# Layer B of a two-layer encoder: fewer, wider steps for the norms of queries and keys, the key scaling on GpSimd, and another order of the steps

## The chip, the core and the metric

One core of one Trainium2 chip runs the whole program: TensorE (PE in the views, its weight loads PEld), VectorE (DVE), ScalarE (ACT), GpSimd (POOL) and SyncE (SP). The metric is the device time of one launch in microseconds (us).

## The reference, cut to what matters

Two layers over 1024 tokens of width 1024. Layer A is sparse attention with an MLP. Layer B, where the change is, is attention with 16 heads whose keys and values come from a 256-wide latent `c_kv` and whose queries come from a 384-wide one `c_q`. Everything is float32.

```python
kv = (c_kv @ w_ukv).reshape(b, s, 16, 64 + 64)          # keys without position, values
k = rms_norm(concat([kv[..., :64], k_rope_of_all_heads]), k_gain)   # 96 wide, root mean square per head and token
q = rms_norm((c_q @ w_uq).reshape(b, s, 16, 96), q_gain)
k, q = rope_tail(k, cos, sin), rope_tail(q, cos, sin)   # the last 32 of 96 are rotated
p = softmax(where(key_chunk <= query_chunk, q @ k.T * 96 ** -0.5, -1e30))
out = x + (p @ v) @ w_o                                 # then an MLP of width 4096
```

## The kernel before

Tokens go in 8 blocks of 128. All products are made from a high and a low part of each operand (the helper of L86 copies the high part on ACT and subtracts on DVE or GpSimd for the low one), three products for each. A first phase of layer B (1439 to 1519 us) makes `c_kv` and `c_q`. Then its attention runs over 8 pairs of heads, j = 0 to 7, each in four quarters u = 0 to 3: (half 0, head 0), (half 1, head 0), (half 0, head 1), (half 1, head 1), where a half is four blocks of queries. About 52 us go to one pair, until 1962 us. The output projection and the last MLP follow.

**A quarter.** `logits` of a block: products `blps` (L930, in pieces of at most 512 columns, two buffers), a DVE pass that copies them to `bpr` and takes the row extreme into `bsm` (L931), the exponential on ACT (L934), the reciprocal of its sum on DVE (L935), and the scaling of the row by it on GpSimd (L936). In the next quarter `values` transposes these rows (`bpt`, L949), splits them (`bph`, `bpl`, L86), and multiplies by the values (`bpo`, L954); `output` adds the result to `res` (L963, L964). A transpose `bpt` of four blocks needs the fourth block's row last, that of `bpr_…_3`, 1024 wide in half 1.

**Beside it**, steps for later pairs are spread between those of the quarter, in the order of `plan` (`first_plan` for pair 0):

- `kv_a(j, t2)`: keys and values of pair j for two blocks. Products `pukv` (L744), a copy of the keys to `ktok` (L749), then four ACT squares with a running sum, `ksq` (L755, one for each block and head, each followed by a read of the accumulator), into `bkss`; then the inverse root. `rsqrt` (L77 to L82) is on DVE: `ms`, then `y` = `ms` to the power -1/2 on GpSimd (L78), and three small DVE passes over `t` and one over `y` (L79 to L82). Last the keys are multiplied by it on DVE (L759, 256 elements, and L760, the 128 of the rotated part).
- `kv_b`: transposes of `ktok` (`pkt`, L769) and their split to `kth`, `ktl`.
- `q_a(j, t2)`: products `puq` (L788), copy to `qtok` (L792), four squares `bqsq` (L796) with accumulators. `q_b(j, half)`: inverse roots for four blocks (`ms_bq`, `y_bq`, `t_bq`), scaling and rotation (L807 to L813; on GpSimd for j > 0, else on DVE). `queries_t`: transposes `pqt` (L819).

Each engine works off its own queue in the order in which the instructions stand there; the framework that builds the program fixes that order, and an engine whose next instruction waits does nothing else meanwhile.

## Time and profile before

| | |
|---|---|
| three runs, us | 2758.19, 2761.0, 2764.25; median 2761.0 |
| profiled execution, us from its first to its last instruction | 2760.2 |
| layer B: first phase / attention / output projection / MLP, us | 80 / 443 / 90 / 708 |
| PE busy in these, us | 79.8 / 405.4 / 86.6 / 700.2 |

The page gives the profiled execution's span, 2760.2 us, and no time around it; the median of the runs is 0.8 us above it. A stage in which PE is busy nearly all of the time can be shortened by less PE work alone; elsewhere it is the time that PE stands still that could go, and what it stands still for is in the waits.

### The profile page before, as it was taken

What the parts mean: (1) busy time and instruction counts of PE and PEld (TensorE: products, weight loads), DVE (VectorE), ACT (ScalarE), POOL (GpSimd) and SP (SyncE); (2) the same over time, 40 slices, a digit from 0 to 9 for tenths busy, and PEclk for the clock granted to TensorE, in tenths of its full rate; (3) what the DMA queues carried; (4) which work ended last, traced back from release to release, by engine and by line L of the source; (5) the groups of instructions that cost most, each with busy time, mean ns of one, the idle gap of its engine ahead of it and who ended that gap; (6) DMA issues with size and microseconds to landing.
All of it is one profiled execution on the core that took longest, in us unless ns stands there. A gap on an engine that the chain in (4) does not pass through costs nothing.

```text
span 2760.2 us, 37019 instructions
## 1 busy us (share of the span) xinstructions
...
## 2 busy tenths in 40 slices
...
DMA packets 122295, 173.05 MB, mean 63 GB/s; under 512 B 12752, under 2 KB 101104, under 8 KB 122112
## 3 DMA queue, kind: packets, MB, share of 16 engines
...
q14 instruction: 78, 0.64, 0.1%
...
## 4 chain that ended last, share of the span: by engine, by line
PE 52%; DVE 4%; ACT 2%; DMA 1%; issue 1%; POOL 1%; SPq 0%; DVEq 0%; ACTq 0%; POOLq 0%
PE pd L1175 19%; PE pu L1105 19%; PE pwo L1058 2%; PE blps L930 2%; PE bpo L954 2%; PE puq L788 2%; PE bpt L949 1%; PE pukv L744 1%; PE pcq L847 1%; DVE bpr L931 1%; PE pck L847 1%; ACT bpr L934 1%; PE pwob L1058 0%; PE pqt L819 0%; PE pt_m L114 0%
## 5 line engine op out<-in xcount | busy, mean ns | idle before, releaser
L1176 DVE TENSOR_TENSOR res<-res,pd 128x1024 f32<-128x1024 f32 x256 | 310.7, 1218 | 358.7 <-PE pd L1175 358.7
L86 POOL TENSOR_TENSOR dl<-rd,dh 128x1024 fp32r<-128x1024 f32 x96 | 234.5, 2444 | 771.0 <-ACT dh L86 750.2
L1175 PE MATMUL pd<-dh,hh 128*128 128x512 f32 x1024 | 405.4, 396 | 38.1 <-DVE res L1176 25.2
L1105 PE MATMUL pu<-mxh,uh 128*128 128x512 f32 (+1 forms) x1056 | 407.4, 386 | 1.9 <-DVE mxl L86 1.9
L1105 PE MATMUL pu<-mxh,ul 128*128 128x512 f32 (+1 forms) x1056 | 407.0, 385 | 1.6 <-POOL ul L86 1.6
L1105 PE MATMUL pu<-mxl,uh 128*128 128x512 f32 (+1 forms) x1056 | 406.9, 385 | 0.0
L1175 PE MATMUL pd<-dl,hh 128*128 128x512 f32 x1024 | 401.6, 392 | 0.5 <-POOL dl L86 0.5
L1175 PE MATMUL pd<-dh,hl 128*128 128x512 f32 x1024 | 397.1, 392 | 3.3 <-DVE hl L86 3.0
L86 POOL TENSOR_TENSOR ul<-ru,uh 128x1024 fp32r<-128x1024 f32 x96 | 238.6, 2486 | 200.9 <-ACT uh L86 200.8
L86 ACT CAST dh<-rd 128x1024 fp32r<-128x1024 f32 x96 | 100.8, 1054 | 418.8 <-PE pd L1175 344.3
L1175 PEld LDWEIGHTS pd<-dh,hh 128*128 128x128 f32 x1024 | 193.9, 189 | 90.1 <-DVE res L1176 34.0
L1162 ACT ACTIVATE sq<-pu 128x512 f32<-128x512 f32 (+1 forms) x132 | 77.1, 586 | 437.7 <-PE pu L1105 433.7
L86 DVE TENSOR_TENSOR hl<-sq,hh 128x512 fp32r<-128x512 f32 (+1 forms) x132 | 212.0, 1608 | 74.5 <-ACT hh L86 74.5
L1105 PEld LDWEIGHTS pu<-mxh,uh 128*128 128x128 f32 x1056 | 200.8, 190 | 41.6 <-DVE mxl L86 2.4
L1105 PEld LDWEIGHTS pu<-mxh,ul 128*128 128x128 f32 x1056 | 200.8, 190 | 41.3 <-POOL ul L86 2.0
L1105 PEld LDWEIGHTS pu<-mxl,uh 128*128 128x128 f32 x1056 | 200.7, 190 | 39.5
L1175 PEld LDWEIGHTS pd<-dh,hl 128*128 128x128 f32 x1024 | 193.9, 189 | 46.1 <-DVE hl L86 5.4
L1175 PEld LDWEIGHTS pd<-dl,hh 128*128 128x128 f32 x1024 | 194.1, 190 | 40.3 <-POOL dl L86 0.9
L1163 DVE TENSOR_TENSOR sq<-sq 128x512 f32<-128x512 f32 (+1 forms) x132 | 119.8, 909 | 108.5 <-ACT sq L1162 108.2
L442 DVE TENSOR_SCALAR_CACHE_REDUCE both<-score,cand 128x384 f32<-128x384 f32 (+2 forms) x192 | 181.2, 944 | 4.1
L86 ACT CAST hh<-sq 128x512 fp32r<-128x512 f32 (+1 forms) x132 | 80.2, 608 | 186.2 <-DVE sq L1163 185.4
L936 POOL TENSOR_SCALAR bpr<-bpr,bsm 128x640 f32<-128x640 f32 (+7 forms) x128 | 96.9, 763 | 111.5 <-DVE bsm L935 37.7
(384 smaller groups left out, 6104.7 us busy)
## 6 DMA issues: line engine op xcount, KB each, us to landing
...
```

The costliest lines, as they stand in the source:

```text
L86: return self.nc.scalar.copy(h, src), (engine or self.nc.vector).tensor_sub(l, src, h)
L442: nc.vector.tensor_scalar(scratch[0][0][:, :s.shape[-1]], s, cand[:, j:j + 1], None, op0=ALU.is_ge, op1=ALU.add, accum_out=cnt[:, j:j + 1])
L788: nc.tensor.matmul(ps[:, 192 * u:192 * u + 192], a[:, kb, tsl], b[:, kb], start=(kb == 0 and i == 0), stop=(kb == 2 and i == 2))
L847: nc.tensor.matmul(ps, a[:, kb], b[:, kb], start=(kb == 0 and i == 0), stop=(kb == KB - 1 and i == 2))
L930: nc.tensor.matmul(lps, q[0:rows, tsl], k[0:rows, h, c:c + a], start=(m == 0), stop=(m == 2))
L936: nc.gpsimd.tensor_scalar(pr, pr, sm[:, 3:4], 1.0, op0=ALU.mult, op1=ALU.mult)
L954: nc.tensor.matmul(po[:, c], vals[j][:, sb, h], m[:, c], start=(sb == 0 and n == 0), stop=(sb == nb - 1 and n == 1))
L1105: nc.tensor.matmul(pu, a[:, kb], b[:, kb, c0:c1], start=(kb == 0 and i == 0), stop=(kb == KB - 1 and i == 2))
L1162: nc.scalar.activation(sq, pu, AF.Relu)
L1163: nc.vector.tensor_mul(sq, sq, sq)
L1175: nc.tensor.matmul(pd[:, ns], a[:, tsl], b[:, ns], start=(f == 0 and k == 0), stop=(f == NF - 1 and k == 2))
L1176: nc.vector.tensor_add(res[:, tb], res[:, tb], pd)
```

## The change

In layer B alone, and not in its matrix products:

- `kv_a` and `q_a`: one ACT square over all heads of two blocks (256 or 384 elements) into a wider `sq` tile, without an accumulator, and one DVE `tensor_reduce` over it, in place of four squares with accumulators.
- The rest of `kv_a` becomes a step of its own, `kv_n(j, half)`: one inverse root for four blocks (128x8) in place of two (128x4), then the scaling of the keys of those four blocks, on DVE for pair 0 and on GpSimd for all others. `ktok` has four buffers in place of three.
- `plan` and `first_plan` are written anew around it. `kv_a(j+1, 1)` moves from the third quarter to the second, `kv_n(j+1, 0)` stands at the start of the third, `kv_n(j+1, 1)` in the fourth.
- The program is built with `dynamic_dma_scratch_size=1024`. (Comments and docstrings are gone too; line numbers move by up to 7: L930 becomes L937, L931 L938, L936 L943, L949 L956, L759 and L760 become L768 and L769.)

```diff
-                kt = j2.tile([P, 2, 2, 96], F32, name=f"ktok{j}_{t2}", tag="ktok", bufs=3)
-                ss = j2.tile([P, 2, 2], F32, name=f"bkss{j}_{t2}", tag="bkss")
+                kt = j2.tile([P, 2, 2, 96], F32, name=f"ktok{j}_{t2}", tag="ktok", bufs=4)
+                if t2 % 2 == 0:
+                    sums["k", j, t2 // 2] = j2.tile([P, 4, 2], F32, name=f"bkss{j}_{t2}", tag="bkss")
...
-                for u in range(2):
-                    for h in range(2):
-                        junk = j2.tile([P, 96], F32, name=f"ksq{j}_{t2}_{u}_{h}", tag="junk")
-                        nc.scalar.activation(junk[:, 0:64], kt[:, u, h, 0:64], AF.Square, accum_out=ss[:, u, h:h + 1])
-                nc.vector.tensor_add(ss, ss, krs[:, 2 * t2:2 * t2 + 2].unsqueeze(2).to_broadcast([P, 2, 2]))
-                r = self.rsqrt(j2, ss.rearrange("p a b -> p (a b)"), 4, 96, f"bk{j}_{t2}")
-                r4 = r.rearrange("p (a b) -> p a b", a=2).unsqueeze(3)
-                nc.vector.tensor_tensor(kt[:, :, :, 0:64], kt[:, :, :, 0:64], r4.to_broadcast([P, 2, 2, 64]), op=ALU.mult)
-                nc.vector.tensor_tensor(kt[:, :, :, 64:96], krp[:, 2 * t2:2 * t2 + 2].unsqueeze(2).to_broadcast([P, 2, 2, 32]),
-                                        r4.to_broadcast([P, 2, 2, 32]), op=ALU.mult)
+                sq = j2.tile([P, 2, 2, 64], F32, name=f"ksq{j}_{t2}", tag="junk", padded_shape=[P, 2, 2, 96])
+                nc.scalar.activation(sq, kt[:, :, :, 0:64], AF.Square)
+                b = 2 * (t2 % 2)
+                nc.vector.tensor_reduce(sums["k", j, t2 // 2][:, b:b + 2], sq, axis=AX.X, op=ALU.add)
                 keys[j, t2] = kt
+
+            def kv_n(j, half):
+
+                eng = nc.gpsimd if j > 0 else nc.vector
+                ss = sums.pop(("k", j, half))
+                nc.vector.tensor_add(ss, ss, krs[:, 4 * half:4 * half + 4].unsqueeze(2).to_broadcast([P, 4, 2]))
+                r = self.rsqrt(j2, ss.rearrange("p a b -> p (a b)"), 8, 96, f"bk{j}_{half}").rearrange("p (a b) -> p a b", a=4)
+                for t2 in (2 * half, 2 * half + 1):
+                    kt, b = keys[j, t2], 2 * (t2 % 2)
+                    r4 = r[:, b:b + 2].unsqueeze(3)
+                    eng.tensor_tensor(kt[:, :, :, 0:64], kt[:, :, :, 0:64], r4.to_broadcast([P, 2, 2, 64]), op=ALU.mult)
+                    eng.tensor_tensor(kt[:, :, :, 64:96], krp[:, 2 * t2:2 * t2 + 2].unsqueeze(2).to_broadcast([P, 2, 2, 32]),
+                                      r4.to_broadcast([P, 2, 2, 32]), op=ALU.mult)
...
-                for u in range(2):
-                    for h in range(2):
-                        junk = j2.tile([P, 96], F32, name=f"bqsq{j}_{t2}_{u}_{h}", tag="junk")
-                        nc.scalar.activation(junk, q[:, u, h], AF.Square, accum_out=sums[j, half][:, b + u, h:h + 1])
+                sq = j2.tile([P, 2, 2, 96], F32, name=f"bqsq{j}_{t2}", tag="junk")
+                nc.scalar.activation(sq, q, AF.Square)
+                nc.vector.tensor_reduce(sums[j, half][:, b:b + 2], sq, axis=AX.X, op=ALU.add)
...
-                [(kv_a, 1, 0), (queries_t, 1, 0, 0), (q_a, 2, 1)],
-                [(q_w, 3), (kv_a, 1, 1), (kv_b, 1, 0), (q_b, 2, 0), (queries_t, 1, 1, 0), (q_a, 2, 2)],
-                [(kv_a, 1, 2), (kv_b, 1, 1), (queries_t, 1, 0, 1), (kv_a, 1, 3), (q_a, 2, 3)],
+                [(kv_a, 1, 0), (queries_t, 1, 0, 0), (kv_a, 1, 1), (q_a, 2, 1)],
+                [(kv_n, 1, 0), (q_w, 3), (q_b, 2, 0), (kv_b, 1, 0), (queries_t, 1, 1, 0), (q_a, 2, 2)],
+                [(kv_a, 1, 2), (kv_b, 1, 1), (kv_a, 1, 3), (queries_t, 1, 0, 1), (kv_n, 1, 1), (q_a, 2, 3)],
...
-                0: [(q_b, 0, 1), (kv_a, 0, 3), (kv_b, 0, 2), (q_b, 1, 0), (queries_t, 0, 1, 0), (kv_w, 1), (kv_b, 0, 3), (q_w, 2),
-                    (queries_t, 0, 1, 1)],
-                1: [(q_b, 1, 1), (kv_a, 1, 0), (q_a, 2, 0), (queries_t, 1, 0, 0), (q_a, 2, 1)],
+                0: [(q_b, 0, 1), (kv_a, 0, 3), (kv_n, 0, 1), (q_b, 1, 0), (kv_b, 0, 2), (queries_t, 0, 1, 0), (kv_w, 1), (kv_b, 0, 3),
+                    (q_w, 2), (queries_t, 0, 1, 1)],
+                1: [(q_b, 1, 1), (kv_a, 1, 0), (q_a, 2, 0), (kv_a, 1, 1), (queries_t, 1, 0, 0), (q_a, 2, 1)],
```

In the first phase `kv_n(0, 0)` is put behind `kv_a(0, 1)`.

What this does to the queues is shown at two places of pair 3; pairs 2 to 5 have the same order there. A name gives pair, half, head and block, so `bpr3_1_0_3` is the row of the fourth block of half 1, head 0, of pair 3; the number at its end is the buffer's.

**The start of the third quarter.** On GpSimd before, from the second block of the quarter that ends to the first of the one that begins:

```order
L936 TENSOR_SCALAR bpr3_1_0_1_16873<-bpr3_1_0_1_16873,bsm3_1_0_1_16874 128x768
L78 TENSOR_TENSOR y_bk4_0_16916<-ms_bk4_0_16915,mhalf_65 128x4
L936 TENSOR_SCALAR bpr3_1_0_2_16936<-bpr3_1_0_2_16936,bsm3_1_0_2_16937 128x896
L78 TENSOR_TENSOR y_bq5_0_17177<-ms_bq5_0_17176,mhalf_65 128x8
L936 TENSOR_SCALAR bpr3_1_0_3_16967<-bpr3_1_0_3_16967,bsm3_1_0_3_16968 128x1024
L936 TENSOR_SCALAR bpr3_0_1_0_17021<-bpr3_0_1_0_17021,bsm3_0_1_0_17022 128x128
```

and of the change, the same stretch:

```order
L943 TENSOR_SCALAR bpr3_1_0_1_16600<-bpr3_1_0_1_16600,bsm3_1_0_1_16601 128x768
L78 TENSOR_TENSOR y_bk4_0_16780<-ms_bk4_0_16779,mhalf_65 128x8
L943 TENSOR_SCALAR bpr3_1_0_2_16646<-bpr3_1_0_2_16646,bsm3_1_0_2_16647 128x896
L78 TENSOR_TENSOR y_bq5_0_16849<-ms_bq5_0_16848,mhalf_65 128x8
L768 TENSOR_TENSOR ktok4_0_16628<-ktok4_0_16628,y_bk4_0_16780 128x4x64
L769 TENSOR_TENSOR ktok4_0_16628<-krp_12616,y_bk4_0_16780 128x4x32
L768 TENSOR_TENSOR ktok4_1_16705<-ktok4_1_16705,y_bk4_0_16780 128x4x64
L769 TENSOR_TENSOR ktok4_1_16705<-krp_12616,y_bk4_0_16780 128x4x32
L943 TENSOR_SCALAR bpr3_1_0_3_16677<-bpr3_1_0_3_16677,bsm3_1_0_3_16678 128x1024
L943 TENSOR_SCALAR bpr3_0_1_0_16746<-bpr3_0_1_0_16746,bsm3_0_1_0_16747 128x128
```

Both inverse roots (L78) stand ahead of the scaling of `bpr3_1_0_3` in either; of the change the four key scalings stand there as well, behind `y_bq`.

On PE before, from the last product of that block's logits to the first transpose that reads its row (repeated products left out):

```order
L930 MATMUL blps3_1_0_3_512_16974<-kth1_14073,qtl10_14082 128x512
L954 MATMUL bpo3_0_0_16861<-bpl3_0_0_3_16985,bv3_15884 128x128
L744 MATMUL pukv4_1_17088<-ukh4_16712,ckh_12612 128x256
...
L949 MATMUL bpt3_1_0_1_17067<-ident_58,bpr3_1_0_1_16873 128x128
L744 MATMUL pukv4_1_17088<-ukh4_16712,ckl_12613 128x256
L949 MATMUL bpt3_1_0_2_17126<-ident_58,bpr3_1_0_0_16846 128x128
L949 MATMUL bpt3_1_0_2_17126<-ident_58,bpr3_1_0_1_16873 128x128
L930 MATMUL blps3_0_1_0_0_17023<-kth1_14073,qth01_14077 128x128
...
L930 MATMUL blps3_0_1_2_0_17080<-kth1_14073,qtl01_14081 128x384
L769 MATMUL pkt4_0_17147<-ident_58,ktok4_0_16901 96x128 x4
L930 MATMUL blps3_0_1_3_0_17139<-kth1_14073,qth01_14077 128x512
...
L949 MATMUL bpt3_1_0_0_17032<-ident_58,bpr3_1_0_3_16967 128x128
```

and of the change:

```order
L937 MATMUL blps3_1_0_3_512_16684<-kth1_13995,qtl10_14004 128x512
L937 MATMUL blps3_0_1_0_0_16748<-kth1_13995,qth01_13999 128x128
...
L956 MATMUL bpt3_1_0_3_16864<-ident_58,bpr3_1_0_0_16573 128x128
L956 MATMUL bpt3_1_0_3_16864<-ident_58,bpr3_1_0_2_16646 128x128
L937 MATMUL blps3_0_1_1_0_16770<-kth1_13995,qth01_13999 128x256
...
L937 MATMUL blps3_0_1_2_0_16805<-kth1_13995,qth01_13999 128x384
...
L937 MATMUL blps3_0_1_3_0_16840<-kth1_13995,qth01_13999 128x512
...
L937 MATMUL blps3_1_1_0_0_16957<-kth1_13995,qth11_14001 128x320
...
L956 MATMUL bpt3_1_0_0_16757<-ident_58,bpr3_1_0_3_16677 128x128
```

The 12 products `pukv4_1` and the transposes `pkt4_0` no longer stand in between (the former are now ahead of this stretch, the latter behind it); `blps3_1_1_0_0` has come in.

On DVE before, from the last row pass of that block on:

```order
L931 ISA bpr3_1_0_3_16967,bsm3_1_0_3_16968<-blps3_1_0_3_512_16974,zero_14092,bsm3_1_0_3_16968 128x512
L81 TENSOR_SCALAR t_bk4_0_16917<-t_bk4_0_16917 128x4
L77 TENSOR_SCALAR ms_bq5_0_17176<-bqss5_0_16817 128x8
L82 TENSOR_TENSOR y_bk4_0_16916<-y_bk4_0_16916,t_bk4_0_16917 128x4
L964 TENSOR_TENSOR res_69<-bpo3_0_0_16861,btmp3_0_0_16990 64x4x128
L759 TENSOR_TENSOR ktok4_0_16901<-ktok4_0_16901,y_bk4_0_16916 128x4x64
L935 RECIPROCAL bsm3_1_0_3_16968<-bsm3_1_0_3_16968 128x1
L931 ISA bpr3_0_1_0_17021,bsm3_0_1_0_17022<-blps3_0_1_0_0_17023,zero_14092 128x128
```

and of the change:

```order
L938 ISA bpr3_1_0_3_16677,bsm3_1_0_3_16678<-blps3_1_0_3_512_16684,zero_14014,bsm3_1_0_3_16678 128x512
L803 TENSOR_REDUCE bqss5_0_16549<-bqsq5_1_16743 128x4
L938 ISA bpr3_0_1_0_16746,bsm3_0_1_0_16747<-blps3_0_1_0_0_16748,zero_14014 128x128
L81 TENSOR_SCALAR t_bk4_0_16781<-t_bk4_0_16781 128x8
L77 TENSOR_SCALAR ms_bq5_0_16848<-bqss5_0_16549 128x8
L938 ISA bpr3_0_1_1_16768,bsm3_0_1_1_16769<-blps3_0_1_1_0_16770,zero_14014 128x256
L82 TENSOR_TENSOR y_bk4_0_16780<-y_bk4_0_16780,t_bk4_0_16781 128x8
L942 RECIPROCAL bsm3_1_0_3_16678<-bsm3_1_0_3_16678 128x1
```

A reduction, the next block's row pass and a pass of the keys' chain now stand ahead of `ms_bq`, on which `y_bq` on GpSimd waits.

**The start of the next pair's first quarter.** On GpSimd before and of the change:

```order
L78 TENSOR_TENSOR y_bk4_2_17314<-ms_bk4_2_17313,mhalf_65 128x4
L936 TENSOR_SCALAR bpr3_1_1_2_17356<-bpr3_1_1_2_17356,bsm3_1_1_2_17357 128x896
L78 TENSOR_TENSOR y_bk4_3_17438<-ms_bk4_3_17437,mhalf_65 128x4
L936 TENSOR_SCALAR bpr3_1_1_3_17387<-bpr3_1_1_3_17387,bsm3_1_1_3_17388 128x1024
L936 TENSOR_SCALAR bpr4_0_0_0_17479<-bpr4_0_0_0_17479,bsm4_0_0_0_17480 128x128
L936 TENSOR_SCALAR bpr4_0_0_1_17501<-bpr4_0_0_1_17501,bsm4_0_0_1_17502 128x256
```

```order
L78 TENSOR_TENSOR y_bk4_1_17111<-ms_bk4_1_17110,mhalf_65 128x8
L943 TENSOR_SCALAR bpr3_1_1_2_17035<-bpr3_1_1_2_17035,bsm3_1_1_2_17036 128x896
L768 TENSOR_TENSOR ktok4_2_16995<-ktok4_2_16995,y_bk4_1_17111 128x4x64
L769 TENSOR_TENSOR ktok4_2_16995<-krp_12616,y_bk4_1_17111 128x4x32
L768 TENSOR_TENSOR ktok4_3_17063<-ktok4_3_17063,y_bk4_1_17111 128x4x64
L769 TENSOR_TENSOR ktok4_3_17063<-krp_12616,y_bk4_1_17111 128x4x32
L943 TENSOR_SCALAR bpr3_1_1_3_17086<-bpr3_1_1_3_17086,bsm3_1_1_3_17087 128x1024
L943 TENSOR_SCALAR bpr4_0_0_0_17149<-bpr4_0_0_0_17149,bsm4_0_0_0_17150 128x128
```

One inverse root less, and four key scalings more, stand ahead of the scaling of `bpr3_1_1_3`. On PE 17 of the 18 products `puq5_3`, which stood behind the last product of that block's logits, now stand ahead of it.

## Rows read from the trace of the kernel before

**Rows 1.** The page of the profiled execution: its span.

```profile
span 2760.2 us, 37019 instructions
```

**Rows 2.** The view by stretches: from:to in us from the start, length, then busy us (and instructions) of PE, PEld, DVE, ACT and POOL, the granted TensorE clock as a share of full speed, the DMA share and GB/s. The first is the projections of layer B, the next three its attention from the first pair to the eighth (first pair, second, five steady pairs, the last). The last two are short stretches in the first two pairs.

```profile
1439.00:1519.00 80.00, 79.78 (x574) 79.81 (x575) 50.26 (x223) 39.64 (x159) 17.25 (x27) 0.98 0.01 4
1519.00:1562.00 43.00, 30.45 (x204) 27.52 (x204) 34.39 (x102) 25.52 (x106) 23.90 (x24) 0.84 0.06 15
1562.00:1610.00 48.00, 42.06 (x264) 36.35 (x263) 39.07 (x120) 32.30 (x104) 24.49 (x29) 0.89 0.04 12
1610.00:1862.00 252.00, 242.93 (x1654) 212.38 (x1652) 220.35 (x737) 210.10 (x726) 138.22 (x156) 0.99 0.04 10
1862.00:1962.00 100.00, 89.98 (x523) 73.89 (x524) 78.52 (x240) 72.85 (x182) 51.39 (x47) 0.98 0.16 51
...
1536.00:1548.00 12.00, 6.48 (x27) 5.58 (x28) 9.98 (x16) 2.25 (x5) 10.28 (x11) 0.50 0.08 23
1570.70:1573.70 3.00, 2.99 (x11) 2.59 (x11) 1.74 (x4) 1.90 (x4) 1.11 (x2) 0.50 0.00 0
```

**Rows 3.** The view of waits for 1526 to 1962: engine, tile and line that waited, what it waited for, us in total, times, the longest. The last row is the same view for the five steady pairs alone (1610 to 1862).

```profile
PE blps L930 <- DVE bsm L931: 11.9, 24, 2.9
...
PE blps L930 <- DVE bsm L931: 5.9, 17, 0.7
```

**Rows 4.** The view by tile for 1610 to 1862 (five pairs, 20 passes of kv_a), one row for all instructions that write or read a tile; the columns with a number are busy us (and instructions) of the engines named here: ksq on DVE and ACT; bqsq on ACT; bkss on DVE; t_bk on DVE; t_bq on DVE.

```profile
1610.00:1862.00 252.00, 0.00 (x0) 23.42 (x160) 0.99 0.04 10
1610.00:1862.00 252.00, 24.03 (x157) 0.99 0.04 10
1610.00:1862.00 252.00, 10.10 (x40) 0.99 0.04 10
1610.00:1862.00 252.00, 23.49 (x79) 0.99 0.04 10
1610.00:1862.00 252.00, 7.95 (x36) 0.99 0.04 10
```

**Rows 5.** The view by line and shape for 1610 to 1862: line, engine, operation, out<-in, shape, count | busy us, mean ns of one | idle before. Two copies on ACT, then GpSimd, then DVE.

```profile
L749 ACT COPY ktok<-pukv 128x256 f32<-128x256 f32 x20 | 7.3, 367 | 0.6 <-PE pukv L744 0.4
L792 ACT COPY qtok<-puq 128x384 f32<-128x384 f32 x19 | 9.0, 473 | 3.1 <-PE puq L788 2.8
L807 POOL TENSOR_TENSOR qtok<-qtok,y_bq 128x768 f32<-128x768 f32 x9 | 13.2, 1472 | 1.2 <-DVE ms_bk L77 0.7 <-DVE y_bq L82 0.5
L811 POOL TENSOR_TENSOR qtok<-qtok,tn 128x512 f32<-128x512 f32 x9 | 12.1, 1340 | 0.2
L812 POOL TENSOR_TENSOR qtok<-qtok,tq 128x256 f32<-128x256 f32 x9 | 6.6, 733 | 0.9 <-DVE rot L810 0.9
L759 DVE TENSOR_TENSOR ktok<-ktok,y_bk 128x256 f32<-128x256 f32 x19 | 7.9, 417 | 0.2
L760 DVE TENSOR_TENSOR ktok<-krp,y_bk 128x128 f32<-128x128 f32 x19 | 5.4, 282 | 0.0
L931 DVE CUSTOM_DVE_ANT_0 bpr<-blps,zero 128x384 f32<-128x384 f32 x20 | 11.0, 549 | 0.7 <-PE blps L930 0.5
```

**Rows 6.** The timeline of the first pair, PE and DVE: start, us, engine, line, operation, out<-in, shape, and the idle time ahead of it with what ended it.

```profile
1544.01 1.06 PE L769 MATMUL pkt<-ident,ktok 128*96 128x128 f32 x4 [4.52 <-DVE ktok L760]
1537.56 1.43 DVE L79 TENSOR_TENSOR t_bk<-ms_bk,y_bk 128x4 f32<-128x4 f32 x1 [0.78 <-POOL y_bk L78]
...
1567.12 0.66 PE L949 MATMUL bpt<-ident,bpr 128*128 128x128 f32 x4 [1.21 <-POOL bpr L936]
1570.71 0.64 PE L930 MATMUL blps<-kth,qth 104*128 104x320 f32 x1 [2.94 <-DVE bsm L931]
1567.91 1.47 DVE L759 TENSOR_TENSOR ktok<-ktok,y_bk 128x256 f32<-128x256 f32 x1
```

**Rows 7.** The timeline of a steady pair about the start of its third quarter: PE, DVE, POOL.

```profile
1671.22 0.23 PE L954 MATMUL bpo<-bpl,bv 128*128 128x128 f32 x1
1671.28 0.33 PE L744 MATMUL pukv<-ukh,ckh 128*128 128x256 f32 x1
1672.62 0.38 PE L949 MATMUL bpt<-ident,bpr 128*128 128x128 f32 x2
1674.59 0.44 PE L930 MATMUL blps<-kth,qth 104*128 104x384 f32 x1 [0.26 <-DVE bsm L931]
1676.12 0.50 PE L930 MATMUL blps<-kth,qth 104*128 104x512 f32 x1 [0.23 <-DVE bsm L931]
1676.92 0.49 PE L949 MATMUL bpt<-ident,bpr 128*128 128x128 f32 x3
1672.71 0.16 DVE L77 TENSOR_SCALAR ms_bq<-bqss 128x8 f32<-128x8 f32 x1
1672.96 1.64 POOL L78 TENSOR_TENSOR y_bq<-ms_bq,mhalf 128x8 f32<-128x8 f32 x1 [1.11 <-DVE ms_bq L77]
1674.59 1.13 POOL L936 TENSOR_SCALAR bpr<-bpr,bsm 128x1024 f32<-128x1024 f32 x1
```

**Rows 8.** The timeline about the start of the next pair's first quarter: PE, POOL.

```profile
1696.43 0.29 PE L954 MATMUL bpo<-bpl,bv 128*128 128x256 f32 x1
1701.41 0.49 PE L949 MATMUL bpt<-ident,bpr 128*128 128x128 f32 x3
1699.74 1.13 POOL L936 TENSOR_SCALAR bpr<-bpr,bsm 128x1024 f32<-128x1024 f32 x1
```

4 lines of the change are left out of this document (2 added, 2 removed).

## The prediction

> **What bounds the kernel now.** I read the view by stretches first, since a mean over the program says little here. PE is busy for 79.8 of 80 us in layer B's projections, so the part of the change that falls there (a new `kv_n(0, 0)`, fewer squares) lies under PE and gives nothing [rows 2]; with PE's cover gone it would cost its own microsecond or two on ACT and DVE, which stand at 39.6 and 50.3 of 80. All that can move is the 443 us of attention. There PE stands still for 12.6 us in the first pair, 5.9 in the second, 9.1 in the five steady pairs together (1.8 us each) and 10.0 in the last [rows 2]: 37.6 us, which is the most that could be had, apart from what the clock gives. The waits say for what: row passes on DVE that come late (`bsm`), 11.9 us in all, 5.9 in the steady pairs [rows 3]; and in the first pair single long stalls, 4.5 us for `ktok`, then 1.2 and 2.9 us for a scaled row and for a row pass [rows 6]. The clock adds to it: 1536 to 1548 and 1570.7 to 1573.7, right behind these stalls, run at 0.50, the lower of its two levels [rows 2].
>
> **What the change removes and adds, per pair.** ACT: four squares with their accumulator reads take 23.42/20 = 1.17 us a pass for keys and 24.03/19.6 = 1.22 for queries [rows 4]; four passes of each are 9.6 us. The wide squares are not in the trace; the copies of the same 256 and 384 elements take 0.37 and 0.47 [rows 5], so 3.4 us come back: −6.2 us of 42. DVE: the keys' chain takes (10.10 + 23.49)/20 = 1.68 us, four times 6.7 [rows 4]. Two wide ones, at the queries' price of 7.95/9 = 0.88 plus 0.51 for the first two steps, are 2.8. The scaling that leaves is 4 x 0.70 = 2.8 [rows 5]. Eight reductions of 256 or 384 elements come in, which the trace does not have: not under the 0.28 of a 128-element pass, hardly over the 0.42 and 0.55 of passes of their own size [rows 5], so 2.2 to 3.9; I take 3.4, near the passes of the same size. Net −3.3 us (−2.8 to −4.5) of 44. GpSimd: 128 elements of scaling are not in the trace. A line through `qtok` with 512 and 256 elements (1.34, 0.73) gives 0.73 + 0.43 for a pass of keys; the slope of the 768-element one, whose second operand is repeated in the same way, gives 0.58 + 0.35 [rows 5]. Four instructions are thus 1.85 to 2.33 us; I take 2.1, the middle, as both shapes occur. PE's products stay the same.
>
> The Trainium skill, "GPSIMD Engine Reference", section "Elementwise — side-by-side cycle accounting", has GpSimd 1.96 times as slow as DVE in a two-input pass; by that the four would take 2 x 1.96 x 0.70 = 2.7 us, and the forecast below would be some 4 us longer. The trace's own pairs of sizes say less.
>
> So DVE and ACT, which are late now, get lighter, and GpSimd, busy for 27.6 of 50 us in a steady pair, gets heavier. That would be a plain gain if nothing waited for GpSimd. The order says that something does.
>
> **Third quarter, pairs 2 to 5.** Count from E, when the last product of the fourth block's logits has gone out (1671.22 in the pair shown [rows 7]). Before, `ms_bq` runs at E+1.5, `y_bq` from E+1.74 to E+3.4, the row `bpr_1_0_3` until E+4.5; PE gets to the transposes that need it only at E+5.7, with 0.49 us of idle on the way. The change puts a reduction (about 0.45), a 128-wide pass (about 0.3) and a 0.16 step ahead of `ms_bq`, but no longer a held `t_bk`: `y_bq` starts at E+2.0 to E+2.65, I take E+2.2. Then 1.64 for it, 2.1 for the four key scalings, which now stand ahead of the row, 1.13 for the row: E+7.1. On PE the twelve `pukv` (1.4 us by [rows 7]) and four `pkt` (about 0.4) that filled this time are gone, and about 0.4 of logits came in: it arrives at 5.7 − 1.4 − 0.4 + 0.4 = E+4.3, or E+3.8 if the idle 0.49 goes. It then stands still for about 3.3 us. Less the 0.49 of before: +2.9 us, four times **+11.6**. Bounds: 2.0 with cheap scalings and late PE, 3.9 with dear ones.
>
> **First quarter of the next pair, three times.** The keys' scaling waits for the last step of its chain, which DVE now reaches behind the last pass of the old row, two passes of the new quarter and the `res` sum (estimates by 0.55 for 384 columns [rows 5]: 0.7, 0.3, 0.4 and 0.7, with 0.9 for a chain of four steps and 0.5 of waiting for products in between): about E'+3.5; plus 2.1 and 1.13 is E'+6.7, where the row was done at E'+4.4 before and PE came at E'+5.0 [rows 8]. PE has lost 17 `puq` of cover (1.9 us), but its logits wait for the same row passes. Between 0 (these hold PE as long) and 3.7 I take 1.4, nearer the former: **+4.2**.
>
> **First pair.** `pkt` stood still for 4.5 us because the chain from 1537.56 on was stretched: its first step took 1.43 us, and a scaling at 1567.91 took 1.47, against means of 0.30 and 0.42 [rows 4 to 6]. The new order ends this chain for four blocks at once, ahead of the queries' GpSimd work that lay beside it: −2.5 (−1 to −4). The 1.2 and 2.9 us before 1570.71 came from a chain and two scalings ahead of a row pass; those scalings leave DVE: −3 (0 to −4.1). The lower clock behind it goes with it: 3 us at 0.50 are 1.5 us lost, −1.5. The 3.99 us ahead of it stay, since the queries of pair 0 are not touched. Together **−7**.
>
> **Other waits.** Of 9.1 us in the steady pairs I let the lighter DVE take 3.5, of 10.0 at the end 2.5: **−6** (0 to −14).
>
> **Clock.** Stalls of 2.9 us and more were followed by the lower level [rows 2, 6]. If each second of the four new ones is, at 1.5 us: **+3** (0 to +12).
>
> Sum: 11.6 + 4.2 − 7 − 6 + 3 = +5.8 on the span of 2760.2 [rows 1], so 2766.0; the median of the runs stood 0.8 above the span: **2767 us**. 0.2%, 5.5 us, is about what a measurement of this kernel can tell from no change.
>
> **The rivals.**
> (a) GpSimd holds PE, as above: 2767, its own range 2761 to 2776. Chance 0.38.
> (b) The relief carries, faster: GpSimd gets its scalings done before PE asks, since 1.1 us of idle stood ahead of `y_bq` [rows 7]. It decides at bpr done by E+4.3, which needs the scalings behind the row or `y_bq` 2.8 us earlier; or the first pair gives back far more. Then −7 − 6 and up to −9 more of the idle: 2740 to 2755, about 2748. For it speaks that DVE is what PE waits for now [rows 3]; against it that the order on GpSimd is fixed. Chance 0.34.
> (c) Both cancel: 2756 to 2766. Chance 0.18.
> (d) The clock falls behind every new stall, seven of them at up to 3 us: 2776 to 2790. For it the two stretches at 0.50. Chance 0.10.
> A rule that speaks for (a) or (d): the Trainium skill, "SBUF — State Buffer", section "Who interferes with whom", says that a DVE pass with two SBUF inputs and a GpSimd instruction that reads SBUF block each other, the later one until the first is done. The stretched `t_bk` of 1.43 us agrees [rows 6]. By that rule the queries' chain would run into the four scalings on GpSimd at each head and DVE would give back about 1.2 us each time, two thirds of its relief; the time would be near 2771.
>
> Within 0.2% (2755.5 to 2766.5) are (c) and a quarter of (a): 0.27. Faster: (b) and a little of (c), 0.36. Slower: the rest of (a) and (d), 0.37. The range of 2746 to 2782 leaves out the lower third of (b) and the upper half of (d).
>
> **What the next profile would show.** Right: PE waits for `bpr` on GpSimd at the transposes grow from 1.2 us to 10 or more, in single stalls of about 3 us at the third quarters of pairs 2 to 5; DVE in 1610 to 1862 falls from 44 to about 41 a pair, ACT from 42 to 36, GpSimd rises to about 31; `pkt` no longer waits 4.5 us in the first pair. Wrong: no such stalls, `y_bq` early or the key scalings far under 1.85 us for four, PE idle in the steady pairs under 1.8 us each.

## The result, and the profile after

The changed kernel takes **2788.9 us** (median of 4 runs, 2783.1 to 2790.1) against 2761.7 of the kernel before (4 runs, 2758.2 to 2764.3) beside it: 1.0100 times as long, 95% interval 1.0087 to 1.0112. The forecast was 2767 within 2746 to 2782. The sign of its likeliest case was right, with 0.37 given to slower and 0.36 to faster; the time lies above the range.

The page of the profiled run gives its span, which answers to [rows 1]: 27.8 us more.

```profile
span 2788.0 us, 36514 instructions
```

The view by stretches (from:to, length, busy us and instructions of PE, PEld, DVE, ACT and POOL, granted clock, DMA share, GB/s), first of after: from the first logits of pair 2 to the first of pair 6, and the whole attention. Then of before: the whole attention and pairs 2 to 5, cut at the same instructions.

```profile
1649.00:1876.00 227.00, 205.50 (x1341) 178.57 (x1340) 184.95 (x555) 149.69 (x361) 125.24 (x153) 0.95 0.04 10
1533.00:1993.00 460.00, 409.50 (x2587) 353.95 (x2586) 365.57 (x1095) 302.06 (x715) 256.09 (x295) 0.94 0.07 20
```

```profile
1529.00:1963.00 434.00, 399.36 (x2589) 344.66 (x2588) 365.27 (x1179) 334.57 (x1086) 236.00 (x253) 0.96 0.07 20
1646.00:1852.00 206.00, 198.24 (x1342) 172.57 (x1341) 180.54 (x597) 169.69 (x576) 114.92 (x128) 0.99 0.04 11
```

The attention is 26 us longer. PE does the same products (2587 records, 2589 before), so its 10.1 us of extra busy time are slower products (granted clock 0.94 for 0.96), and the other 15.9 us are idle time (50.5 for 34.6, each the length less PE's busy time). In pairs 2 to 5 the split is 7.3 and 13.7 of 21 us. ACT has become lighter by 32.5 us in the attention; DVE's busy time has not moved in all (365.6 for 365.3); in pairs 2 to 5, which take 21 us more, it rose by 4.4 us (185.0 for 180.5).

The waits of PE in 1526 to 2000, and the first row of the same view for pairs 2 to 5 (1649 to 1876). Before, `bpt` waited for `bpr` once, for 1.2 us [rows 6], and the longest sum was the 11.9 us for `bsm` [rows 3].

```profile
PE bpt L956 <- POOL bpr L943: 17.7, 13, 2.9
PE blps L937 <- DVE bsm L938: 8.5, 17, 1.5
...
PE pkt L777 <- DVE ktok L769: 5.8, 1, 5.8
...
PE bpt L956 <- POOL bpr L943: 14.5, 8, 2.9
```

One of these stalls, at the start of the third quarter of pair 3 (the place of [rows 7], one pair on): PE, then DVE, then POOL.

```profile
1735.21 0.23 PE L937 MATMUL blps<-kth,qth 104*128 104x128 f32 x1
...
1739.21 0.31 PE L937 MATMUL blps<-kth,qtl 96*128 96x320 f32 x1
1742.10 0.86 PE L956 MATMUL bpt<-ident,bpr 128*128 128x128 f32 x4 [2.58 <-POOL bpr L943]
1743.80 0.63 PE L961 MATMUL bpo<-bph,bv 128*128 128x512 f32 x1
1744.22 0.63 PE L961 MATMUL bpo<-bpl,bv 128*128 128x512 f32 x1
...
1737.89 0.16 DVE L942 RECIPROCAL bsm<-bsm 128x1 f32<-128x1 f32 x1
...
1737.43 1.65 POOL L78 TENSOR_TENSOR y_bq<-ms_bq,mhalf 128x8 f32<-128x8 f32 x1 [2.02 <-DVE ms_bq L77]
1739.05 0.61 POOL L768 TENSOR_TENSOR ktok<-ktok,y_bk 128x256 f32<-128x256 f32 x1
1739.62 0.40 POOL L769 TENSOR_TENSOR ktok<-krp,y_bk 128x128 f32<-128x128 f32 x1
1739.97 0.61 POOL L768 TENSOR_TENSOR ktok<-ktok,y_bk 128x256 f32<-128x256 f32 x1
1740.54 0.40 POOL L769 TENSOR_TENSOR ktok<-krp,y_bk 128x128 f32<-128x128 f32 x1
```

The reciprocal of the row's sum is there at 1738.05, but GpSimd has `y_bq` and four scalings ahead of it and takes it at 1740.92; PE stands from 1739.52 to 1742.10. Behind the stall the products of 512 columns come 0.42 us apart, and the granted clock is near 0.50, the lower level (1.2 of 2.4 GHz). It is so behind all four stalls of 2.57 to 2.87 us at the third quarters of pairs 2 to 5 (PE, then the stretches behind them):

```profile
1684.45 1.11 PE L956 MATMUL bpt<-ident,bpr 128*128 128x128 f32 x4 [2.87 <-POOL bpr L943]
1799.92 0.67 PE L956 MATMUL bpt<-ident,bpr 128*128 128x128 f32 x4 [2.58 <-POOL bpr L943]
1856.93 0.66 PE L956 MATMUL bpt<-ident,bpr 128*128 128x128 f32 x4 [2.57 <-POOL bpr L943]
...
1684.50:1687.90 3.40, 3.40 (x13) 2.98 (x14) 2.66 (x6) 2.59 (x6) 3.40 (x6) 0.52 0.00 0
1742.50:1745.90 3.40, 3.40 (x14) 2.73 (x12) 2.67 (x7) 2.92 (x6) 3.40 (x5) 0.51 0.02 5
1800.50:1803.90 3.40, 3.33 (x12) 2.85 (x12) 2.46 (x7) 2.74 (x6) 3.40 (x5) 0.51 0.01 2
1858.50:1861.90 3.40, 3.37 (x13) 2.70 (x12) 2.97 (x6) 2.22 (x5) 3.17 (x4) 0.50 0.02 5
1687.90:1742.50 54.60, 48.98 (x336) 42.55 (x335) 44.64 (x136) 35.62 (x89) 29.11 (x36) 1.00 0.04 11
```

The last row is the time between two of them: with no wait over 1.00 us in it, the clock stays full.

Per shape, in pairs 2 to 5, the new operations cost (DVE, ACT, ACT, DVE, then the two scalings on GpSimd; to be read against [rows 5]; the second figure behind the bar is the mean in ns):

```profile
L803 DVE TENSOR_REDUCE bqss<-bqsq 128x4 f32<-128x384 f32 x16 | 8.7, 547 | 0.2 <-ACT bqsq L802 0.2
L802 ACT ACTIVATE bqsq<-qtok 128x384 f32<-128x384 f32 x15 | 7.9, 524 | 0.3
L754 ACT ACTIVATE ksq<-ktok 128x256 f32<-128x256 f32 x15 | 6.5, 436 | 0.0
L756 DVE TENSOR_REDUCE bkss<-ksq 128x4 f32<-128x256 f32 x15 | 6.1, 408 | 0.0
...
L768 POOL TENSOR_TENSOR ktok<-ktok,y_bk 128x256 f32<-128x256 f32 x16 | 9.8, 612 | 5.9 <-DVE y_bk L82 5.9
L769 POOL TENSOR_TENSOR ktok<-krp,y_bk 128x128 f32<-128x128 f32 x16 | 6.4, 398 | 0.0
```

So the stalls that the prediction's first rival described are there. The question for the experiments was whether they are the 27 us.

### The profile page after: what moved, and what is told of

Its sections match the earlier page's. It is cut to its first block, busy times and chain, and to the rows that moved or that the text cites. A ratio compares the mean times of both kernels' runs of the same rounds, so it can differ in the third digit from the quotient of the medians.

```text
span 2788.0 us, 36514 instructions
## 1 busy us (share of the span) xinstructions
PE 2576.8 (92%) x13354; PEld 2173.9 (78%) x13354; DVE 1874.9 (67%) x3996; ACT 1132.4 (41%) x2409; POOL 1045.6 (38%) x796
## 3 DMA queue, kind: packets, MB, share of 16 engines
q8 instruction: 105, 1.72, 0.3%
## 4 chain that ended last, share of the span: by engine, by line
PE 52%; DVE 4%; POOL 2%; issue 1%; DMA 1%; ACT 1%; SPq 0%; DVEq 0%; ACTq 0%; POOLq 0%
PE pd L1182 18%; PE pu L1112 18%; PE pwo L1065 3%; PE blps L937 2%; PE bpo L961 2%; PE puq L796 2%; PE pukv L744 1%; PE bpt L956 1%; PE pcq L854 1%; PE pck L854 1%; DVE bpr L938 1%; POOL bpr L943 1%; DMA ukr<-in_w_ukv_dram 1%; PE pqt L826 0%; PE pkt L777 0%
## 5 line engine op out<-in xcount | busy, mean ns | idle before, releaser
L1182 PEld LDWEIGHTS pd<-dh,hh 128*128 128x128 f32 x1024 | 194.9, 190 | 90.8 <-DVE res L1183 34.6
L943 POOL TENSOR_SCALAR bpr<-bpr,bsm 128x640 f32<-128x640 f32 (+7 forms) x128 | 94.6, 747 | 102.7 <-DVE bsm L942 59.4
```

What stands on the lines that cost most here:

```text
L943: nc.gpsimd.tensor_scalar(pr, pr, sm[:, 3:4], 1.0, op0=ALU.mult, op1=ALU.mult)
L1182: nc.tensor.matmul(pd[:, ns], a[:, tsl], b[:, ns], start=(f == 0 and k == 0), stop=(f == NF - 1 and k == 2))
```

## The experiments

Ratios are to the kernel before, run beside each, with 95% intervals. Line numbers of a kernel's rows are its own.

**Undo one part of the change at a time.** The first four runs leave out or keep one part each: the scaling on GpSimd, the new order of steps, or all but one.

e1, against the changed kernel:

```diff
-                eng = nc.gpsimd if j > 0 else nc.vector
+                eng = nc.vector
```

> The changed kernel with one word changed: the keys are scaled on DVE for every pair, not on GpSimd for all but the first. Its order on PE about the third quarter's start is that of the changed kernel (no pukv and no pkt between the last logits of the fourth block and the transposes that need its row); on GpSimd only the two inverse roots stand ahead of that row. Theory A (the four scalings on GpSimd ahead of the row hold PE): the row is done 2.0 us earlier at some ten heads, PE's waits for bpr on GpSimd fall from 17.7 us to under 6, the lower clock behind them goes for the most part, and the time is 2764 to 2772. Theory B (the steps' new order took the products away that covered this time, whichever engine scales): 2779 to 2788, since the lost cover stays lost and DVE gets 2.8 us a pair back.

2784.1 us, 1.0087 (1.0071 to 1.0104). With the keys scaled on DVE again PE's waits for GpSimd's rows fall from 17.7 us to 4.4, none over 0.8, but other waits take their place (PE's longest sums in 1526 to 2000; the changed kernel has 8.5 for `bsm`):

```profile
PE blps L937 <- DVE bsm L938: 17.4, 32, 1.5
PE bpt L956 <- DVE ktl L86: 7.0, 6, 1.4
```

By this run the scaling on GpSimd is worth 4 or 5 of the 27 us.

e2, against the changed kernel: the plan of before, with `kv_n` behind each second `kv_a`.

```diff
-                [(kv_a, 1, 0), (queries_t, 1, 0, 0), (kv_a, 1, 1), (q_a, 2, 1)],
-                [(kv_n, 1, 0), (q_w, 3), (q_b, 2, 0), (kv_b, 1, 0), (queries_t, 1, 1, 0), (q_a, 2, 2)],
+                [(kv_a, 1, 0), (queries_t, 1, 0, 0), (q_a, 2, 1)],
+                [(q_w, 3), (kv_a, 1, 1), (kv_n, 1, 0), (kv_b, 1, 0), (q_b, 2, 0), (queries_t, 1, 1, 0), (q_a, 2, 2)],
...
```

> The changed kernel with the plan of before (kv_a in its old places, each kv_n right behind its second kv_a); the scaling stays on GpSimd. Now the scalings stand behind the long rows of both heads on GpSimd, and the twelve pukv cover the third quarter's start again. Theory A and theory B both expect the heads' stalls to be gone: 2752 to 2765. Theory C (GpSimd as such is too full, or its key scalings slow DVE through the memory they share, wherever they stand): 2775 to 2788, with DVE passes of two inputs stretched as much as in the changed kernel.

2790.6 us, 1.0116 (1.0095 to 1.0137): the old plan brings nothing back. Under it the keys come late (PE waits 13.0 us in 9 stalls for `ktok` on GpSimd).

e3, against the kernel before; the keys' squares likewise.

```diff
-                for u in range(2):
-                    for h in range(2):
...
-                        nc.scalar.activation(junk, q[:, u, h], AF.Square, accum_out=sums[j, half][:, b + u, h:h + 1])
+                sq = j2.tile([P, 2, 2, 96], F32, name=f"bqsq{j}_{t2}", tag="junk")
+                nc.scalar.activation(sq, q, AF.Square)
+                nc.vector.tensor_reduce(sums[j, half][:, b:b + 2], sq, axis=AX.X, op=ALU.add)
```

> The kernel before with one part of the change: wide squares on ACT and reductions on DVE, the inverse roots for two blocks, scaling on DVE and plan as before. If the relief of ACT (6.2 us a pair) and the small extra of DVE (3.4 us a pair) are what the first step of the prediction said, it is within 2752 to 2764. If the reductions on DVE delay the row passes, over 2766.

2775.8 us, 1.0059 (1.0041 to 1.0076). The wide squares with their reductions, which I had netted inside DVE's sum, cost 15 us alone.

e4, against the kernel before; the scaling of the other 128 elements likewise.

```diff
-                nc.vector.tensor_tensor(kt[:, :, :, 0:64], kt[:, :, :, 0:64], r4.to_broadcast([P, 2, 2, 64]), op=ALU.mult)
+                eng = nc.gpsimd if j > 0 else nc.vector
+                eng.tensor_tensor(kt[:, :, :, 0:64], kt[:, :, :, 0:64], r4.to_broadcast([P, 2, 2, 64]), op=ALU.mult)
```

> The kernel before with one part of the change: the keys are scaled on GpSimd for all but the first pair, two blocks at a time, plan and squares as before. About the third quarter's start two scalings (1.0 us) stand ahead of the long row on GpSimd, and the twelve pukv still cover it. Theory A: PE reaches the row about when it is done, 2758 to 2768. Theory C: over 2770.

2760.3 us, 1.0000 (0.9991 to 1.0009). Moving 2.8 us a pair from DVE to GpSimd neither costs nor gives anything under the plan of before.

**Squares or reductions, and is a lighter engine worth anything?**

x1, against the kernel before; x4 has the first two lines alone.

```diff
+                red = j2.tile([P, 2, 2], F32, name=f"kred{j}_{t2}", tag="kred")
+                nc.vector.tensor_reduce(red, kt[:, :, :, 0:64], axis=AX.X, op=ALU.add)
...
+                red = j2.tile([P, 2, 2], F32, name=f"qred{j}_{t2}", tag="kred")
+                nc.vector.tensor_reduce(red, q, axis=AX.X, op=ALU.add)
```

> The kernel before with eight more DVE reductions a pair (0.41 and 0.55 us each, 3.8 us a pair), whose results nothing reads; the squares on ACT, the order of the products and all else as before. Theory D (DVE is the engine that PE waits for, and each reduction that stands in its queue ahead of row passes and splits is paid for): 2770 to 2780, as the kernel with squares and reductions (2775.8). Theory O (not DVE's load costs, but the new order of PE's products that the framework makes when ACT's squares get short): 2760 to 2765.

2776.3 us, 1.0062 (1.0046 to 1.0079), as e3: eight reductions a pair that nobody reads cost 17 us, with ACT's squares as they were. What PE waits for (1526 to 2000) is passes on DVE, of which `bpl` has grown (the third row is of before):

```profile
PE bpo L958 <- DVE bpl L86: 10.8, 19, 1.6
PE blps L934 <- DVE bsm L935: 10.7, 17, 2.9
...
PE bpo L954 <- DVE bpl L86: 3.6, 11, 0.7
```

> The kernel before with four more DVE reductions a pair in place of eight, those over the keys (0.41 us each, 1.6 us a pair), results unused. In proportion to eight (3.8 us a pair, 15 us): 2766. If there is slack that the first ones use up: 2760 to 2763.

2770.1 us, 1.0033 (1.0023 to 1.0044): about 10 us for the four of the keys, whose work is 1.6 us a pair by the row of the 256-element reduction above, 13 in all; x1 pays 17 for some 30.

x2 and x3, against the kernel before. x2 has one wide square with one accumulator for all heads of a pass and no reduction; x3 leaves out the 256-element scaling of the keys for all pairs but the first.

```diff
+                s1 = j2.tile([P, 1], F32, name=f"bks1{j}_{t2}", tag="bks1")
+                nc.scalar.activation(sq, kt[:, :, :, 0:64], AF.Square, accum_out=s1)
...
+                if j == 0:
+                    nc.vector.tensor_tensor(kt[:, :, :, 0:64], kt[:, :, :, 0:64], r4.to_broadcast([P, 2, 2, 64]), op=ALU.mult)
```

> The kernel before with one wide square in place of four in each pass and no reductions: the accumulator of the one square stands for all four sums (so the norms of keys and queries in layer B are other numbers than the reference's). DVE's work is that of before, ACT loses about 4.5 us a pair; the twelve pukv still stand behind the fourth block's last logits. Theory D: 2750 to 2760, what the relief of ACT is worth by itself. Theory O: over 2765.

2757.2 us, 0.9995 (0.9984 to 1.0005). In 1610 to 1862 ACT is busy for 185.3 us instead of the 210.1 of [rows 2], and nothing is gained.

> The kernel before without the wider of the two passes that scale the keys (0.42 us, four a pair) for all pairs but the first, so that these keys are not normalised in 64 of 96 columns; nothing takes its place, the order on PE is that of before. If each microsecond of DVE counts alike, up and down: 1.7 us a pair less give 6 to 7 us, 2752 to 2755. If DVE only bounds once more work is put on it: 2757 to 2761.

2763.8 us, 1.0011 (1.0001 to 1.0020). DVE 1.7 us a pair lighter, and no gain. So e4, x2 and x3 give no sign of the "relief" of my sum. They don't show that it is worth nothing: none of them keeps the order of before. Against the trace of before, at least 217, 356 and 170 of PE's 13354 instructions stand in another place, so that a worse order may have eaten a gain.

**The order of single steps.**

e5, against the changed kernel:

```diff
-                [(kv_n, 1, 0), (q_w, 3), (q_b, 2, 0), (kv_b, 1, 0), (queries_t, 1, 1, 0), (q_a, 2, 2)],
+                [(q_w, 3), (q_b, 2, 0), (kv_n, 1, 0), (kv_b, 1, 0), (queries_t, 1, 1, 0), (q_a, 2, 2)],
```

> The changed kernel with one step moved: kv_n of the third quarter stands behind q_b, by which its scalings stand behind the long row on GpSimd there (in the first quarter they still stand ahead). Theory A (the scalings ahead of the row are what costs): the stalls of 2.6 us at the third quarters and the lower clock behind them go, 2770 to 2776. If DVE's reductions and the lost cover cost instead, as the kernel with all keys on DVE says: 2780 to 2790.

2796.8 us, 1.0134 (1.0119 to 1.0149): slower still, and PE's waits for `bpr` on GpSimd stay (18.8 us in 11, for 17.7 in 13).

e7 is e2 with the scaling on DVE; y1 is the kernel before with the keys' roots for four blocks at once and nothing else (accumulators on ACT, scaling on DVE, old plan).

> The changed kernel with the plan of before and all keys scaled on DVE: of the change only squares, reductions and the inverse roots for four blocks are left. Against the kernel with squares and reductions alone (2775.8) it shows what the inverse roots for four blocks cost, against the changed kernel with keys on DVE (2784.1) what the plan costs. If the plan costs: 2772 to 2778. If keys that wait for four blocks cost: 2782 to 2788, with PE waiting for pkt's keys.

2788.0 us, 1.0101 (1.0085 to 1.0116), with 13.4 us of waits for `ktok`, 5.8 of them in one stall that the changed kernel has as well.

> The kernel before with the inverse roots for four blocks alone: squares with accumulators on ACT, no reductions, keys scaled on DVE, plan of before with each kv_n behind its second kv_a. DVE loses about 3.9 us a pair (two chains of 1.4 in place of four of 1.7). If DVE's load is all that counts (15 us for 3.8 us a pair more): about 2745. Theory W (keys that wait for the second two blocks come late for their transposes, and the chain, the scalings and the queries' chain fall together): 2766 to 2775, with PE waiting for keys at pkt.

2770.4 us, 1.0038 (1.0028 to 1.0049), with 15.7 us in 12 waits of `pkt` for `ktok` (6.1 in 2 before): under the old plan, keys that wait for four blocks come late. The new plan is there to mend that.

y2, against the changed kernel; the queries' squares likewise.

```diff
-                sq = j2.tile([P, 2, 2, 64], F32, name=f"ksq{j}_{t2}", tag="junk", padded_shape=[P, 2, 2, 96])
-                nc.scalar.activation(sq, kt[:, :, :, 0:64], AF.Square)
...
-                nc.vector.tensor_reduce(sums["k", j, t2 // 2][:, b:b + 2], sq, axis=AX.X, op=ALU.add)
+                for u in range(2):
+                    for h in range(2):
...
+                        nc.scalar.activation(junk[:, 0:64], kt[:, u, h, 0:64], AF.Square, accum_out=sums["k", j, t2 // 2][:, b + u, h:h + 1])
```

> The whole change but for one part: the four squares with accumulators stay on ACT, so that there are no reductions on DVE. If the reductions' 15 us add to the rest: 2770 to 2776. If the rest alone is as slow (the scalings on GpSimd ahead of the long rows, the new plan): over 2780. If the change is good but for the reductions: under 2757.

2763.9 us, 1.0017 (1.0008 to 1.0027). Everything else in the change costs 4 or 5 us; with the wide squares and their reductions it costs 27. The build option `dynamic_dma_scratch_size` is in y2 and in x2 as well, so it is not the loss. At the place of the stall shown above, GpSimd now takes the row first (POOL, DVE, PE of y2):

```profile
1726.38 1.13 POOL L945 TENSOR_SCALAR bpr<-bpr,bsm 128x1024 f32<-128x1024 f32 x1 [1.07 <-DVE bsm L944]
1727.61 0.61 POOL L769 TENSOR_TENSOR ktok<-ktok,y_bk 128x256 f32<-128x256 f32 x1
...
1729.82 1.65 POOL L78 TENSOR_TENSOR y_bq<-ms_bq,mhalf 128x8 f32<-128x8 f32 x1
...
1729.19 0.34 DVE L77 TENSOR_SCALAR ms_bq<-bqss 128x8 f32<-128x8 f32 x1
...
1727.57 0.66 PE L958 MATMUL bpt<-ident,bpr 128*128 128x128 f32 x4
```

But the source of y2 does not say so: its steps stand in the same plan. The framework that records the kernel orders the instructions of each engine itself, and with eight instructions a pair more on DVE and fewer on ACT it had made another order on every engine: in the traces of y2 and of the change at least 376 of PE's 13354 instructions and 66 of GpSimd's 796 stand in different places. So the runs up to here mix two causes, DVE's work and the order.

**Work and order apart.** At the end of the recording each instruction gets an edge to the one that is to stand ahead of it on its engine (order only, no wait), from a table of another kernel's order; the reductions alone are free. In this way f1 has x1's reductions in the order of before, g1 the order of x1 and no reduction, f2 the changed kernel in y2's order, and g2 y2 in the changed kernel's order. In the traces each of the four has on PE, DVE, ACT and GpSimd the sequence that it was to have, instruction by instruction, reductions and squares apart.

```diff
+        order = ORDER[e]
+        row = [i for u in order for i in us[u]]
+        for a, b in zip(row, row[1:]):
+            tc.add_manual_dep(b, a.name, no_sync, reason="impose")
```

> The kernel before with eight unused reductions a pair on DVE, as in x1 (2776.3 us), but with the instructions of PE, DVE, ACT and GpSimd held in exactly the order that they have in the kernel before; only the reductions are new among them. Load theory (the 3.8 us of reductions a pair on DVE make the row passes late): about 2776 us, ratio 1.006, and PE waits for bpl and bsm on DVE as in x1 (10.8 and 10.7 us). Order theory (the framework puts the products of layer B in a worse order once the reductions are there): 2760 us, ratio 1.000.

2765.1 us, 1.0021 (1.0011 to 1.0031). PE's waits for `bpl` are near those of before: 4.3 us in 12, for 3.6 in 11.

> The other half of the same test: the kernel before without any reduction, its instructions on the four engines held in the order that they have in x1. Load theory: about 2760 us, ratio 1.000. Order theory: about 2776 us, ratio 1.006. If both halves lie between, each cause has the share that its half shows.

2769.3 us, 1.0035 (1.0022 to 1.0049). Of x1's 17 us about 6 are work on DVE and about 10 the order. The waits for `bpl` that x1 seemed to owe to its reductions are here without one:

```profile
PE bpo L954 <- DVE bpl L86: 10.1, 17, 1.6
```

No run holds a kernel in its own order alone, so what the edges themselves cost is not measured; f1's 6 and g1's 10 us together don't exceed x1's 17, which leaves them little.

> The changed kernel with its reductions and wide squares, its instructions held in the order that they have in y2_change_without_reductions (2763.9 us), so that on GpSimd the scalings of the keys stand behind the row bpr at the third quarter. Load theory: near the changed kernel's 2788 us, ratio 1.010. Order theory: near 2764 us, ratio 1.002.

2771.7 us, 1.0041 (1.0026 to 1.0056): with the reductions, in y2's order, 7 us over y2 and 17 under the changed kernel.

> y2 (accumulators on ACT, no reduction on DVE) with its instructions held in the order of the changed kernel, so that the scalings of the keys stand ahead of the row bpr at the third quarter. Load theory: near 2764 us, ratio 1.002. Order theory: near 2788 us, ratio 1.010, with stalls of some 2.6 us for bpr on GpSimd at the heads of the third quarter.

2789.7 us, 1.0107 (1.0092 to 1.0122): the changed kernel's order costs the whole 27 us without a single reduction, 25 us more than y2. Its longest sum of waits in 1526 to 2000 is that of the changed kernel (17.7 us in 13):

```profile
PE bpt L958 <- POOL bpr L945: 17.9, 14, 2.9
PE blps L939 <- DVE bsm L940: 11.8, 20, 1.5
```

**Is it the four stalls at GpSimd's row?** The last two runs keep the changed kernel's own order and move four instructions of GpSimd, the rows `bpr2_1_0_3` to `bpr5_1_0_3`: in h3 ahead of `y_bq` and the scalings, in h4 between them.

In GpSimd's order, h3 for pair 3:

```diff
 L943 TENSOR_SCALAR bpr3_1_0_2<-bpr3_1_0_2,bsm3_1_0_2 128x896
+L943 TENSOR_SCALAR bpr3_1_0_3<-bpr3_1_0_3,bsm3_1_0_3 128x1024
 L78 TENSOR_TENSOR y_bq5_0<-ms_bq5_0,mhalf 128x8
 L768 TENSOR_TENSOR ktok4_0<-ktok4_0,y_bk4_0 128x4x64
...
-L943 TENSOR_SCALAR bpr3_1_0_3<-bpr3_1_0_3,bsm3_1_0_3 128x1024
```

> The changed kernel (2788 us) held in its own order, with one thing moved: at the third quarters of pairs 2 to 5, GpSimd's row bpr_1_0_3 stands ahead of y_bq and the four scalings instead of behind them, four instructions moved in all. Nothing moves on PE, DVE or ACT. Theory that GpSimd's order at these four places is the loss: the row starts at about 1738.05 instead of 1740.92 in the pair whose stall ends at 1742.10, the four stalls of up to 2.6 us and the lower clock behind them go, so 2770 to 2776 us, ratio 1.004 to 1.006. Theory that the order of the products on PE is the loss: 2784 to 2788 us, ratio 1.009 to 1.010.

2789.1 us, 1.0115 (1.0098 to 1.0132): nothing comes back. GpSimd's row is in time now, and PE stands still longer one step on, behind the four transposes (PE, DVE, POOL of h3 at the same place):

```profile
1733.99 0.64 PE L937 MATMUL blps<-kth,qth 104*128 104x320 f32 x1 [3.45 <-DVE bsm L938]
...
1731.47 0.57 DVE L79 TENSOR_TENSOR t_bq<-ms_bq,y_bq 128x8 f32<-128x8 f32 x1 [1.98 <-POOL y_bq L78]
1732.43 0.54 DVE L81 TENSOR_SCALAR t_bq<-t_bq 128x8 f32<-128x8 f32 x1
1733.25 0.68 DVE L938 CUSTOM_DVE_ANT_0 bpr<-blps,zero 128x512 f32<-128x512 f32 x1
...
1728.71 1.12 POOL L943 TENSOR_SCALAR bpr<-bpr,bsm 128x1024 f32<-128x1024 f32 x1 [2.73 <-DVE bsm L942]
1729.80 1.65 POOL L78 TENSOR_TENSOR y_bq<-ms_bq,mhalf 128x8 f32<-128x8 f32 x1
```

The row pass on DVE that frees the bank for the next logits stands behind the queries' chain (`t_bq`, three more steps), and its first step waits for `y_bq`, now the later one on GpSimd: 1.98 us of idle DVE and 1.8 of chain, ahead of a pass that PE waits for. The stall is the queries' inverse root on two in-order queues; which of the two ends it depends on what stands first on GpSimd.

> As h3, but the row stands behind y_bq and ahead of the four scalings alone, so that only what the change put there (2.02 us of scalings) is moved, and y_bq (1.65 us) stays ahead as in the kernel before. Theory that the scalings ahead of the row are the loss: the four stalls shrink from about 2.6 to 0.6 us, 8 us of idle and some of the lower clock come back, 2774 to 2780 us, ratio 1.005 to 1.007. Theory of the products on PE: 2784 to 2788 us.

2789.6 us, 1.0115 (1.0099 to 1.0130). The stall for `bpr` falls to 0.72 us; one of 0.91 for the row pass and one of 3.03 for `bpl` on DVE come in behind it, the last of these:

```profile
1743.43 0.50 PE L961 MATMUL bpo<-bpl,bv 128*128 128x512 f32 x1 [3.03 <-DVE bpl L86]
```

**What stays open.** Most of the loss is the order of the instructions, as g2 and f2 show, and moving four places on GpSimd alone gives none of it back, as h3 and h4 show. Which places make it is open: whether the place of the chain on DVE would give it back, or that of the products on PE, which no longer cover it, was not tried. Why the framework's order comes out so once reductions are there is not in the trace.

## Why the prediction was right or wrong

Two steps of the prediction failed. It counted a lighter DVE ("Net −3.3 us") as time that PE gets back, and outside the two places that it read it took the order of the instructions to stay as it was (pair 1 at nothing, the last pairs at −2.5). The runs show that the new order costs 25 us without a reduction (g2 against y2), and that DVE did not get lighter.

The forecast's sum against the trace, by the time of the first logits of a pair (1529.13 and 1532.86 for pair 0, before and after; 1592.55 and 1590.17 for pair 1; 1646.39 and 1648.66 for pair 2; 1851.94 and 1876.21 for pair 6; last value product 1963.15 and 1993.11). The stretches of [rows 2] are not cut there: 1562 to 1610, called the second pair, is the end of pair 0 and the start of pair 1, and 1610 to 1862 goes from pair 1 into pair 6.

| stretch | forecast, us | measured, us |
| --- | --- | --- |
| up to pair 0 | 0 | +3.7, of which 2.4 ahead of layer B's projections |
| pair 0 | −7 | −6.1 |
| pair 1 | 0 | +4.7 |
| pairs 2 to 5 | +11.6 +4.2 −3.5 +3 = +15.3 | +22.0 |
| pairs 6 and 7 | −2.5 | +5.7 |
| behind the attention | 0 | −2.1 |
| sum | +5.8 | +27.9 |

Of the first row, what lies ahead of the projections is no work of the change: up to there both programs run the same products in the same order. Single executions differ so; in h3 and h4, which share that part, pair 0 begins at 1523.9 and 1527.2.

- **Third and first quarters, +11.6 and +4.2: right in place, releaser and size.** PE waits for `bpr` on GpSimd 14.5 us in pairs 2 to 5, against 15.8. They are four stalls of 2.6 to 2.9 us at the third quarters (2.9 was forecast, four scalings of 2.02 for 2.1) and four of 1.0 at the first quarters (three of 1.4). With the slower products, 7.3 us, they make up nearly all that these pairs lost. The forecast has a slip here: 3.3 less 0.49 is 2.8, so its term should be 11.2. In the stall shown, with E at 1735.21, `y_bq` starts at E+2.2 (the value taken), PE comes at E+4.3 (the same) and the row is done at E+6.8 (7.1). It does not follow that the scalings are the cause of the loss: with them on DVE (e1, in another order again) the time falls by 5 us, with them behind the row (h3, h4) not at all. Rival (b) put the point from which the relief would carry at a row done by E+4.3; in h3 it is done 4.1 us after E, and nothing carries.
- **"Net −3.3 us" of DVE a pair: the first step that failed.** The prices of the new operations were right (reductions 3.8 a pair, forecast 3.4 with 3.9 as the bound; squares 0.52 and 0.44 for 0.47 and 0.37), but DVE did not get lighter. In pairs 2 to 5 it is busy for 46.2 us a pair, 45.1 before. Its passes for the queries, which run beside GpSimd's (last section), became dearer: the four steps of their chain take 1.48 us for 0.86 and the two passes of the rotation 1.72 for 0.98, 2.7 us a pair more in all. The second pass of the rotation after, and before:

```profile
L817 DVE TENSOR_TENSOR rot<-qtok,sgq 128x128 f32<-128x128 f32 x8 | 8.8, 1095 | 0.0
L810 DVE TENSOR_TENSOR rot<-qtok,sgq 128x128 f32<-128x128 f32 x8 | 3.3, 418 | 0.0
```

  Nor can work in a queue taken in order be netted; it counts by its place. The reductions cost 6 us in the order of before (f1), 7 in x1's (x1 against g1) and 7 in y2's (f2 against y2), and nothing in the change's own (the change against g2); in the last two cases ACT's lighter squares came with them.
- **"Other waits, −6": wrong in sign, the second step that failed.** Pair 1 and pairs 6 and 7, which I priced at 0 and −2.5, lost 4.7 and 5.7. The sum took the order of the rows it quoted at two places and let the rest of the program stand as it was. The change had moved instructions on every engine, and this order costs 25 us without the reductions (g2 against y2) and 17 with them (the change against f2). In y2's order the work on DVE is about 7 us (f2 against y2). The two don't add up; that the stalls of the order hide the work is likely, but not shown.
- **Clock, +3: mis-sized.** Slower products cost 10.1 us in the attention, 7.3 of them in pairs 2 to 5. The granted clock falls behind all four of the stalls of 2.6 to 2.9 us, where I took each second one. Rival (d), the clock behind each of seven stalls, forecast 2776 to 2790 at a chance of 0.10 and holds the time, but by luck: the clock fell behind four, and with its 7.3 us for 3 my sum gives 2771. The rest came from pairs 1, 6 and 7 and from relief that did not come.
- **First pair, −7: right in size (−6.1), in part by luck.** `pkt` still stands still, 5.8 us for 4.5, where −2.5 was forecast. The 1.2 and 2.9 us behind it are gone, as forecast. So are the 4.0 us for `pqt` ahead of it that the forecast let stand, and waits of 1.5, 0.9 and 1.1 us have come in.
- **GpSimd's factor.** The trace's line through other shapes said 2.1 us for four scalings, and that is what they take: 612 to 417 ns on DVE and 398 to 282 are 1.47 and 1.41 times. The Trainium skill, "GPSIMD Engine Reference", section "Elementwise — side-by-side cycle accounting", has 1.96; for these sizes the measurement decides.
- **ACT and GpSimd** went about where forecast (in pairs 2 to 5, ACT 37.4 us a pair for 36, GpSimd 31.3 for 31).
